# A two-layer encoder trunk on one core: projection weights in half loads, and the planner's tables dealt out anew

## The chip, the core and the metric

The kernel runs on one core of a Trainium2 chip. The metric is device time in microseconds for one launch. The core has five engines with instruction streams of their own: TensorE (PE, matmuls and, listed apart as PEld, weight loads), VectorE (DVE), ScalarE (ACT), GpSimd (POOL) and SyncE (SP). SP computes nothing here and issues DMAs, one after the other in the written order; POOL issues those DMAs that add into their target.

## The reference, cut to what matters

The input is 256 frames of 2048 features, all in float32. One layer of forgetting attention and one of chunked attention follow each other, each with an MLP.

```python
h = x
u = rms_norm(h, a_norm_g)                      # layer A
q, k, v, fz = split(u @ a_w_in)                # 16 heads of 128
q, k = rms_norm(q), rms_norm(k)                # per head
s = q k^T * 128**-0.5 + c_t - c_s              # c: running sum of log forget gates, causal
h = h + (softmax(s) @ v) @ a_w_out
h = h + relu(rms_norm(h) @ w1)**2 @ w2         # 2048 -> 8192 -> 2048
k, v = split(rms_norm(h, kv_norm_g) @ kv_w)    # shared keys and values, k normed per head
q = rms_norm(rms_norm(h, b_norm_g) @ b_w_q)    # layer B
h = h + (softmax(q k^T * 128**-0.5 + bias) @ v) @ b_w_out
h = h + relu(rms_norm(h) @ w1)**2 @ w2
```

## The kernel before, in words

**Units.** Every weight is read once, in pieces of 128 x 1024 called units; 972 of them in a fixed order make up the program. Each unit is split into a high part (`hi`, ACT, L287) and the rest (`lo`, DVE, L288), and PE multiplies hi and lo with the activations, which are split in the same way: three groups of four matmuls (L587, L589, L591). `fetch` (L341) keeps the splits AHEAD = 2 units before their matmuls.

**Loads.** `load` (L254) brings weights from DRAM into the pool `wraw` of three buffers of 1 MB, one DMA for a block of two units (L268). Only the first blocks of the program are cut smaller (`parts`, L274). `fetch` asks for blocks until EARLY = 2 blocks stand before their splits.

**Stages.** Layer A: for each of four groups of four heads a panel for Q, one for K and one for V (8 units each, 4 blocks); then the out-projection in four panels; then the MLP; then layer B's query projection; then K and V for layer B (two panels in each group), the second out-projection and the second MLP. MLP and query projection go in pairs of panels. A pair has seven forms f0 to f6 (sums of weight blocks times sums of activations, two steps of six matmuls each, half a unit) and plain units (a, b). The string in ORDER for each kind of pair says in which order forms and plain units come; `r` stands for a plain unit left over from the pair before. The sums of weights are made by adding DMAs on POOL (`add_on`, L317), by a bringing DMA on SP (`bring`, L306) and on DVE (`make`, L326), at places that BEHIND and OPENING set.

**Steps between the units.** All other work is hung behind units by a list, `fill`: after each unit `run_fill` runs the next entry, and `add_fill` and `deal` put work a number of units ahead. The tables are such numbers. HIDDEN places the hidden layer's four moves and six steps, LONG and SHORT the row statistics, the turning (L436), four moves (L451) and four steps of scaling, splitting and summing (L412 to L403) of a group of 512 features; LONG is for the end of layer A, SHORT for the out-projections. The engines DVE, ACT, PE and SP run in the written order (`keep_order`), so a place in the tables is a place in four queues.

**Attention.** `attend` (L782) puts the four heads of a group on steps `at`, and each head's values `far` steps later. Behind step `at` come the score matmuls (L744, L745), one step later bias and maximum on DVE, then the exponential on ACT, then norm and turning on DVE. Then SP writes the 128 x 384 probabilities to DRAM (`rows`, L462, turn<-pbuf) and four DMAs bring them back as columns (`columns`, L468, pbuf<-turn x4). The values (L776, L777) read them. In the table `at` is 9, 12, 15, 18 and `far` 9 for the first three groups, and 8, 10, 12, 13 and 8 for the last, whose values fall into the out-projection's first panel pair.

**Query steps.** `query` (L1020) sets the norms and scalings of layer B's queries by numbers in the code, and with them the flip of the row statistics and the second splitting of the activations for K and V.

Of the kernel before, what the change touches and what calls it, by code (L numbers as in the profile page):

```python
# [22 lines left out]
NG = H // GH  # L23
# [3 lines left out]
NEG = -1.0e30  # L27
UN = 1024
AHEAD = 2
EARLY = 2  # L30
HIDDEN = (
# [4 lines left out]
)  # L36
UA = UN // 512
LONG = (
# [4 lines left out]
)  # L43
SHORT = (
# [4 lines left out]
)  # L49
REL = 384  # L50
ORDER = {
# [9 lines left out]
}  # L61
BEHIND = {
    (0, 0): [(0, 1, "make", 0), (3, 1, "add", "T1", 0)],
    (0, 1): [(0, 1, "make", 1), (4, 1, "add", "T1", 1)],
    (1, 1): [(2, 0, "bring", "12", 0)],
    (3, 1): [(5, 0, "bring", "11", 0), (3, 0, "bring", "11", 1), (6, 0, "add", "T3", 1), (4, 0, "bring", "12", 1)],
    (2, 0): [(3, 0, "add", "T3", 0)],
}
SUBS = {"1": (2, 2), "2": (2, 2), "q": (2, 2)}
OPENING = (  # L70
    (23, "bring", "12", 0),
    (15, "bring", "12", 1),
    (5, "add", "T3", 0),
    (10, "add", "T3", 1),
    (6, "bring", "11", 0),
    (3, "bring", "11", 1),
)
BIG = 2 * UN
FORMS = ("11", "T3", "T2", "T1", "21", "T4", "22")
# [14 lines left out]
def trunk(ctx: ExitStack, tc: tile.TileContext, t):  # L94
# [53 lines left out]

    class Block:

        def __init__(self, src):
            self.src, self.raw = src, None

    def halves_of(src):
        return [(b, s) for b in map(Block, src) for s in range(2)]

    class Item:

# [76 lines left out]
            [(last - 2 + k, q) for k in range(2) for q in range(n)]  # L235

    def stage_units(src, tail):
        u = halves_of(src[i] for i in range(src.shape[0]))
# [8 lines left out]
    units.extend(halves_of(w_kv[i] for i in range(w_kv.shape[0])))  # L247
    tail_b = Tail(stage_units(w_ob, 4))
    plan_b = plan_mlp("b", None, tail_b)
    ready = deque()  # L250
# [3 lines left out]
    def load(parts=0):  # L254
        src, item = units.popleft(), None
        if isinstance(src, Item):
            item = src
            if item.u not in (4, 6):
                raws.append((item, None, (), 0))
                return  # L260
            block, s = item.pair.raw[item.u], item.s
        else:
            block, s = src
        new = block.raw is None
        if new:
            block.raw = wraw.tile([P, block.src.shape[1]], F32, name="raw", tag="raw")
            if not parts:
                SY.dma_start(block.raw, block.src)  # L268
        n = UN // (parts or 1)
        cuts = [slice(i * n, (i + 1) * n) for i in range(parts or 1)]  # L270
        raw = block.raw[:, half(s)]
        if parts:
            for c in cuts:
                SY.dma_start(raw[:, c], block.src[:, half(s)][:, c])  # L274
        raws.append((item, raw, cuts, new))

    def issue():
        if not raws:
            load()
        item, raw, cuts, _ = raws.popleft()  # L280
        if not cuts:
            assert (FORMS[item.u], item.s) in item.pair.done
            raw, cuts = item.pair.t[FORMS[item.u]][:, half(item.s)], [slice(0, UN)]
        hi = wsp.tile([P, UN], F32R, name="hi")
        lo = wsp.tile([P, UN], F32R, name="lo")
        for c in cuts:
            S.activation(hi[:, c], raw[:, c], AF.Copy)  # L287
            V.tensor_tensor(lo[:, c], raw[:, c], hi[:, c].bitcast(F32), op=ALU.subtract)  # L288
        ready.append((hi, lo))
        if item and item.u == 4:  # L290
            add_on(item.pair, "T4", item.s, raw)
        if item:
            item.pair.done.add((item.u, item.s))
            behind(item.pair, item.u, item.s)
        if later:
            for f in later.popleft():
                f()

    def half(s):
        return slice(s * UN, (s + 1) * UN)  # L300
# [5 lines left out]
            SY.dma_start(p.t[name][:, : p.subs * UN], p.big[name])  # L306
        p.done.add((name, s))

    def add_on(p, name, s, raw=None):
        to, block = {"T1": ("11", "12"), "T3": ("12", "22"), "T4": ("T2", "21")}[name]  # L310
        assert (to, s) in p.done
        assert {"T1": {(0, s), ("T2", s)}, "T3": set(), "T4": {(2, s)}}[name] <= p.done
        p.t[name] = p.t[to]
        p.done.add((name, s))
        d = p.t[name][:, half(s)]
        if raw is None:
            G.dma_start(d, p.big[block][:, half(s)], accum_op=ALU.add)  # L317
        else:
            V.tensor_tensor(d, d, raw, op=ALU.add)  # L319

    def make(p, s):
        assert (not p.prev or p.prev.did(5)) and {("T3", s), ("11", s)} <= p.done
# [459 lines left out]
    def attend(g, q, k, v, cq, o, make_bias):  # L782
        st = [{} for _ in range(GH)]
        box = {}
        k4 = k.rearrange("p (i a b c) -> p a b i c", i=4, a=GH, b=NB)
        at, far = ((8, 10, 12, 13), 8) if g == NG - 1 else ((9, 12, 15, 18), 9)
        items = [[] for _ in range(at[-1] + far + 1)]
        step = steps(lambda: make_bias(g, box))
        for i in (3, 6, 7):
# [230 lines left out]
    def query(g):  # L1020
        box = {}

        def f(b, ps):
            if b == 0:
                z, lq = turned(), landing(2 + g % 2)
                box["lq"], box["f"] = lq, head_norm(lambda: st2, z, lq, apart=(0, 2, None, None)[g])
            box["f"](b, ps)
            if b == NB - 1:
                add_fill([[]] * (7 + (2, 4, 0, 0)[g]) + [[lambda: qs.append(scale_q(box["lq"], 1, g))]])
                if g == 1:  # L1030
                    add_fill([[]] * 8 + [[st2.flip]])
                    slots = {0: 0, 1: 0, 2: 1, 3: 1, 4: 2, 5: 2, 6: 3, 7: 3}
                    add_fill([[again[slots[i]]] if i in slots else [] for i in range(8)])
        return f

    again = [steps(lambda n=n: kept[n](True, 2, xkv)) for n in range(NG)]
# [102 lines left out]
```

## Time and profile before

| | |
|---|---|
| runs, us | 2161.41, 2154.07, 2145.67 |
| median, us | 2154.07 |
| the profiled execution's own time, us | 2157.28 |
| its span, us | 2155.5 |
| mean granted clock of PE | 0.992 |
| bytes moved by DMA | 538.85 MB, mean 250 GB/s |

The span runs from the first to the last instruction, and 1.8 us lie around it. Times in timelines are microseconds from the start of the span. In a row of a timeline stand the start, the duration, the engine, the line, the operation, and in brackets the engine's idle time before it and what ended that; SPq is SP's queue of DMA issues, where a duration is time on SP and not the transfer. A row of the list of DMA issues ends with KB each and the median microseconds from issue to landing. Rows of the waits give a total in us, the number of times and the longest.

### The profile page before, as it was taken

The numbers are of one execution on the slowest core, as the hardware profiler recorded it, in microseconds if no ns is written. First come the engines' busy times: TensorE is split into PE (matmuls) and PEld (weight loads), VectorE is DVE, ScalarE is ACT, GpSimd is POOL, SyncE is SP. The second block draws the span as 40 slices with busy tenths as digits, with TensorE's granted clock in tenths as the row PEclk, the third lists the DMA queues.
The fourth block names the chain that finished last, engine by engine and source line by source line (L and its number), as shares of the span: only waits on it lengthen the run. The fifth ranks groups of instructions, "written<-read, shape, count | busy, mean of one in ns | idle before, by whom it ended". The sixth has DMA issues, their size and how long they took to land.

```text
span 2155.5 us, 26474 instructions
## 1 busy us (share of the span) xinstructions
PE 2093.5 (97%) x9114; PEld 1701.9 (79%) x9114; DVE 1735.8 (81%) x2003; ACT 1306.0 (61%) x1567; POOL 166.6 (8%) x184
## 2 busy tenths in 40 slices
PE   9999998999999999999989999989999999999999
PEld 7888886787887887887777888767878878878877
DVE  5767674899889889889898577648898898898896
ACT  6544543767567567557666445446675675675574
POOL 1101000001001000000002000000010010000000
PEclk9999999999999999999999999999999999999999
DMA  8776776888888888889786776758888888888884
GB/s 296 241 247 216 245 251 197 266 267 260 263 277 243 252 289 247 263 266 286 230 243 199 255 231 222 241 181 260 262 250 265 281 250 254 276 257 263 266 285 156
DMA packets 150678, 538.85 MB, mean 250 GB/s; under 512 B 41088, under 2 KB 78096, under 8 KB 101648
## 3 DMA queue, kind: packets, MB, share of 16 engines
q1 hardware_dynamic: 130960, 465.86, 60.5%
q0 software_dynamic: 19584, 71.31, 18.9%
q8 instruction: 71, 1.16, 0.2%
q14 instruction: 63, 0.52, 0.1%
HBM read 497.20 MB, written 15.75 MB: 238 GB/s over the span
## 4 chain that ended last, share of the span: by engine, by line
PE 81%; DVE 6%; DMA 5%; SPq 3%; ACT 3%; issue 2%; DVEq 0%; ACTq 0%; POOLq 0%
PE acc L587 17%; PE acc L589 17%; PE acc L591 17%; PE po L591 5%; PE po L587 5%; PE po L589 5%; PE s L589 4%; PE s L591 4%; PE s L587 4%; DVE lo L288 3%; SPq L451 3%; ACT hi L287 1%; DMA q<-z 1%; DMA pbuf<-turn 1%; DMA turn<-pbuf 1%
## 5 line engine op out<-in xcount | busy, mean ns | idle before, releaser
L288 DVE TENSOR_TENSOR lo<-raw,hi 128x1024 fp32r<-128x1024 f32 (+1 forms) x634 | 759.3, 1214 | 206.0 <-ACT hi L287 202.7
L287 ACT ACTIVATE hi<-raw 128x1024 fp32r<-128x1024 f32 (+1 forms) x634 | 658.5, 1053 | 365.7 <-PE acc L589 199.0
L587 PE MATMUL acc<-hi,act 128*128 128x512 f32 x1644 | 468.3, 401 | 18.9 <-ACT hi L287 9.8
L589 PE MATMUL acc<-hi,act 128*128 128x512 f32 x1644 | 452.9, 392 | 0.0
L591 PE MATMUL acc<-lo,act 128*128 128x512 f32 x1644 | 451.4, 391 | 0.9 <-DVE lo L288 0.9
L587 PEld LDWEIGHTS acc<-hi,act 128*128 128x128 f32 x1644 | 308.4, 190 | 89.7 <-ACT hi L287 13.5
L589 PEld LDWEIGHTS acc<-hi,act 128*128 128x128 f32 x1644 | 311.3, 189 | 67.3 <-DVE act L382 1.1
L591 PEld LDWEIGHTS acc<-lo,act 128*128 128x128 f32 x1644 | 309.3, 189 | 68.6 <-DVE lo L288 3.7
L287 ACT ACTIVATE hi<-w 128x1024 fp32r<-128x1024 f32 x204 | 214.6, 1056 | 104.4 <-PE po L589 52.0
L288 DVE TENSOR_TENSOR lo<-w,hi 128x1024 fp32r<-128x1024 f32 x204 | 245.5, 1221 | 34.5 <-ACT hi L287 32.7
L287 ACT ACTIVATE hi<-wT 128x1024 fp32r<-128x1024 f32 x136 | 142.3, 1057 | 65.0 <-PE po L589 24.9
L288 DVE TENSOR_TENSOR lo<-wT,hi 128x1024 fp32r<-128x1024 f32 x136 | 162.7, 1221 | 20.9 <-ACT hi L287 20.3
L587 PE MATMUL s<-hi,act 128*128 128x512 f32 x476 | 136.4, 391 | 6.5 <-ACT hi L287 4.1
L591 PE MATMUL s<-lo,act 128*128 128x512 f32 x476 | 139.0, 397 | 2.6 <-DVE lo L288 2.6
L589 PE MATMUL s<-hi,act 128*128 128x512 f32 x476 | 136.7, 392 | 1.1 <-DVE act L416 1.1
L587 PEld LDWEIGHTS s<-hi,act 128*128 128x128 f32 x476 | 89.2, 188 | 27.2 <-ACT hi L287 5.3
L591 PEld LDWEIGHTS s<-lo,act 128*128 128x128 f32 x476 | 88.3, 189 | 28.2 <-DVE lo L288 10.8
L589 PEld LDWEIGHTS s<-hi,act 128*128 128x128 f32 x476 | 89.4, 188 | 21.1 <-DVE act L416 2.4
L319 DVE TENSOR_TENSOR wT<-wT,raw 128x1024 f32<-128x1024 f32 x68 | 82.9, 1219 | 0.0
L326 DVE TENSOR_TENSOR wT<-w,w 128x1024 f32<-128x1024 f32 x68 | 82.9, 1219 | 0.0
L779 ACT ACTIVATE act<-po 128x256 fp32r<-128x256 f32 x32 | 12.3, 385 | 102.1 <-PE po L777 102.1
L587 PE MATMUL po<-hi,act 128*128 128x512 f32 x272 | 73.1, 391 | 0.0
(181 smaller groups left out, 2221.6 us busy)
## 6 DMA issues: line engine op xcount, KB each, us to landing
raw<-in_w_in SPq DMA_DIRECT2D x46, 1024.0 KB, 6.2
raw<-in_s1a SPq DMA_DIRECT2D x32, 1024.0 KB, 6.1
raw<-in_s2a SPq DMA_DIRECT2D x32, 1024.0 KB, 7.0
raw<-in_w_kv SPq DMA_DIRECT2D x32, 1024.0 KB, 5.8
raw<-in_s1b SPq DMA_DIRECT2D x32, 1024.0 KB, 5.8
raw<-in_s2b SPq DMA_DIRECT2D x32, 1024.0 KB, 6.2
q<-z SPq DMA_DIRECT2D x672, 32.0 KB, 4.1
raw<-in_w_oa SPq DMA_DIRECT2D x16, 1024.0 KB, 7.1
```

What stands on the lines that cost most here:

```text
L287: S.activation(hi[:, c], raw[:, c], AF.Copy)
L288: V.tensor_tensor(lo[:, c], raw[:, c], hi[:, c].bitcast(F32), op=ALU.subtract)
L319: V.tensor_tensor(d, d, raw, op=ALU.add)
L326: V.tensor_tensor(p.t["T2"][:, half(s)], p.t["T3"][:, half(s)], p.t["11"][:, half(s)], op=ALU.add)
L451: SY.dma_start(d[32 * j : 32 * j + 32, i], z[32 * i : 32 * i + 32, j * n : (j + 1) * n])
L587: TE.matmul(ps, xh, cut(hi, j), start=first, stop=False, **kw)
L589: TE.matmul(ps, xl, cut(hi, j), start=False, stop=False, **kw)
L591: TE.matmul(ps, xh, cut(lo, j), start=False, stop=last, **kw)
L779: S.activation(o[i][:, 0], po[:, :T], AF.Copy)
```

## The change

Weights of the QKV, KV and both output projections are loaded in halves of a block, one DMA of 512 KB for each unit, into the same three buffers of 1 MB; the MLP's and the query's blocks stay whole. EARLY is 4 and counts a half as 1 and a whole block as 2; the first panel's own look-ahead (1) now is a half. The steps of attention and of the query projection become tables (ATT, BIAS, QUERY, AGAIN); BIAS keeps its numbers. T4's sum now is made where BEHIND says, and no more with its block's split. All other tables have new numbers, of which a few stand here:

```diff
-EARLY = 2
+EARLY = 4
 LONG = (
-    (3, 0, 0, 1, 1, 1, 6, 7, 7, 7),
+    (1, 0, 0, 0, 0, 1, 6, 6, 6, 9),
...
 SHORT = (
...
-    (7, 0, 0, 1, 2, 5, 9, 10, 13, 13),
+    (8, 0, 0, 1, 2, 5, 6, 10, 14, 14),
...
+QUERY = (0, 1, 13, 12, 6, 17, 6)
+AGAIN = (0, 1, 2, 3, 5, 5, 7, 7)
+ATT = ((8, 14, 18, 18, 10), (8, 9, 12, 12, 9))
+BIAS = (3, 6, 7)
 ORDER = {
...
-    "q0": "r f0 f1 f2 f3 f4 r a a f5 b f6 b",
-    "q1": "f0 f1 f2 f4 r r a f5 r r a f3 b b f6",
+    "q0": "f0 r f1 r r f2 f3 f4 a a f5 f6 b b",
+    "q1": "f0 f1 r f2 r f4 a f5 r r a r f3 b b f6",
...
-        def __init__(self, src):
-            self.src, self.raw = src, None
+        def __init__(self, src, whole=True):
+            self.src, self.raw, self.whole = src, None, whole
...
-    units.extend(halves_of(w_in[i] for i in range(w_in.shape[0])))
+    units.extend(halves_of((w_in[i] for i in range(w_in.shape[0])), False))
...
-        if parts:
+        if not block.whole:
             for c in cuts:
                 SY.dma_start(raw[:, c], block.src[:, half(s)][:, c])
-        raws.append((item, raw, cuts, new))
+        elif new:
+            SY.dma_start(block.raw, block.src)
+        raws.append((item, raw, cuts, 2 * new if block.whole else 1))
...
-            add_on(item.pair, "T4", item.s, raw)
+            item.pair.t["21", item.s] = raw
...
-        at, far = ((8, 10, 12, 13), 8) if g == NG - 1 else ((9, 12, 15, 18), 9)
+        *at, far = ATT[g == NG - 1]
...
-                add_fill([[]] * (7 + (2, 4, 0, 0)[g]) + [[lambda: qs.append(scale_q(box["lq"], 1, g))]])
+                add_fill([[]] * QUERY[2 + g] + [[lambda: qs.append(scale_q(box["lq"], 1, g))]])
                 if g == 1:
-                    add_fill([[]] * 8 + [[st2.flip]])
+                    add_fill([[]] * QUERY[6] + [[st2.flip]])
+                    deal(AGAIN, [again[i // 2] for i in range(8)])
```

Lines of the kernel after stand 7 lower for most (L268 and L274 become L279, L462 becomes L469, L468 becomes L475). Three places show the order on the engines.

SP at the end of the first attention, where the last group's four heads go out (turn<-pbuf) and come back (pbuf<-turn), between loads for the out-projection (raw). Before:

```order
98 L462 DMA turn<-pbuf 128x384
99 L306 DMA w_2685<-in_f1a 128x2048
100 L468 DMA pbuf<-turn 32x4x96 x4
101 L268 DMA raw<-in_w_oa 128x2048
102 L462 DMA turn<-pbuf 128x384
103 L468 DMA pbuf<-turn 32x4x96 x4
104 L268 DMA raw<-in_w_oa 128x2048
105 L462 DMA turn<-pbuf 128x384
106 L468 DMA pbuf<-turn 32x4x96 x4
107 L462 DMA turn<-pbuf 128x384
108 L268 DMA raw<-in_w_oa 128x2048
109 L468 DMA pbuf<-turn 32x4x96 x4
```

And after:

```order
99 L469 DMA turn<-pbuf 128x384
100 L313 DMA w_2743<-in_f1a 128x2048
101 L279 DMA raw<-in_w_oa 128x1024
102 L475 DMA pbuf<-turn 32x4x96 x4
103 L469 DMA turn<-pbuf 128x384
104 L279 DMA raw<-in_w_oa 128x1024
105 L475 DMA pbuf<-turn 32x4x96 x4
106 L279 DMA raw<-in_w_oa 128x1024 x2
107 L469 DMA turn<-pbuf 128x384 x2
108 L279 DMA raw<-in_w_oa 128x1024
109 L475 DMA pbuf<-turn 32x4x96 x8
```

The last two heads go out one behind the other and come back in one run of eight, and each load between is half as large.

PE in the first query pair, at its forms f0 (s<-hi,act) and f1 (po<-hi,S). Before:

```order
1518 L587 MATMUL s<-hi,act 128x512 x2
1519 L589 MATMUL s<-hi,act 128x512 x2
1520 L591 MATMUL s<-lo,act 128x512 x2
1521 L587 MATMUL po<-hi,S 128x512 x2
1522 L589 MATMUL po<-hi,S 128x512 x2
1523 L591 MATMUL po<-lo,S 128x512 x2
```

And after:

```order
1515 L594 MATMUL s<-hi,act 128x512 x2
1516 L596 MATMUL s<-hi,act 128x512 x2
1517 L598 MATMUL s<-lo,act 128x512 x2
1518 L594 MATMUL acc<-hi,act 128x512 x4
1519 L596 MATMUL acc<-hi,act 128x512 x4
1520 L598 MATMUL acc<-lo,act 128x512 x4
1521 L594 MATMUL po<-hi,S 128x512 x2
```

A plain unit of the last w2 pair (acc) has moved between the two forms; before, it stood ahead of both.

DVE shortly before, in the last w2 pair, where the first group's activations for the query pairs are split (act) and summed (sum, S). Before:

```order
763 L634 TENSOR_TENSOR acc<-acc,p_8437 128x512
764 L288 TENSOR_TENSOR lo<-raw,hi 128x1024 x2
765 L416 TENSOR_TENSOR act<-y,act 128x1024
766 L394 TENSOR_TENSOR sum<-y 128x256
767 L395 TENSOR_TENSOR sum<-y,sum 128x256
768 L396 TENSOR_TENSOR sum<-y 128x256
769 L397 TENSOR_TENSOR sum<-y,sum 128x256
770 L403 TENSOR_TENSOR S<-sum,S 128x512 x2
771 L288 TENSOR_TENSOR lo<-raw,hi 128x1024 x4
```

And after:

```order
758 L641 TENSOR_TENSOR acc<-acc,p_8480 128x512
759 L295 TENSOR_TENSOR lo<-raw,hi 128x1024
760 L423 TENSOR_TENSOR act<-y,act 128x1024
761 L401 TENSOR_TENSOR sum<-y 128x256
762 L402 TENSOR_TENSOR sum<-y,sum 128x256
763 L403 TENSOR_TENSOR sum<-y 128x256
764 L404 TENSOR_TENSOR sum<-y,sum 128x256
765 L295 TENSOR_TENSOR lo<-raw,hi 128x1024 x4
766 L410 TENSOR_TENSOR S<-sum,S 128x512 x2
```

The group's split and sums stand one weight split earlier, and the split of the sums (S) four weight splits later.

More of the change, by code (lines that the diff above doesn't have):

```diff
@@ L71 @@
     (23, "bring", "12", 0),
-    (15, "bring", "12", 1),
-    (5, "add", "T3", 0),
-    (10, "add", "T3", 1),
+    (17, "bring", "12", 1),
+    (4, "add", "T3", 0),
+    (9, "add", "T3", 1),
     (6, "bring", "11", 0),
-    (3, "bring", "11", 1),
+    (1, "bring", "11", 1),
 )
@@ L149, in trunk, with halves_of @@
     class Block:
-        def __init__(self, src):
-            self.src, self.raw = src, None
-    def halves_of(src):
-        return [(b, s) for b in map(Block, src) for s in range(2)]
+        def __init__(self, src, whole=True):
+            self.src, self.raw, self.whole = src, None, whole
+    def halves_of(src, whole=True):
+        return [(b, s) for b in (Block(i, whole) for i in src) for s in range(2)]
     class Item:
@@ L237, in stage_units @@
     def stage_units(src, tail):
-        u = halves_of(src[i] for i in range(src.shape[0]))
+        u = halves_of((src[i] for i in range(src.shape[0])), False)
         u[:16] = [u[8 * q + i] for i, q in steps_of(2)]
@@ L243, in trunk @@
     n_out = 4 * KT // UA - 4
-    units.extend(halves_of(w_in[i] for i in range(w_in.shape[0])))
+    units.extend(halves_of((w_in[i] for i in range(w_in.shape[0])), False))
     tail_a = Tail(stage_units(w_oa, 4))
     plan_a = plan_mlp("a", "qb", tail_a)
-    units.extend(halves_of(w_kv[i] for i in range(w_kv.shape[0])))
+    units.extend(halves_of((w_kv[i] for i in range(w_kv.shape[0])), False))
     tail_b = Tail(stage_units(w_ob, 4))
@@ L307, in bring, with add_on @@
         p.done.add((name, s))
-    def add_on(p, name, s, raw=None):
+    def add_on(p, name, s):
         to, block = {"T1": ("11", "12"), "T3": ("12", "22"), "T4": ("T2", "21")}[name]
         assert (to, s) in p.done
-        assert {"T1": {(0, s), ("T2", s)}, "T3": set(), "T4": {(2, s)}}[name] <= p.done
+        assert {"T1": {(0, s), ("T2", s)}, "T3": set(), "T4": {(2, s), (4, s)}}[name] <= p.done
         p.t[name] = p.t[to]
@@ L315, in add_on @@
         d = p.t[name][:, half(s)]
-        if raw is None:
+        if name == "T4":
+            V.tensor_tensor(d, d, p.t["21", s], op=ALU.add)
+        else:
             G.dma_start(d, p.big[block][:, half(s)], accum_op=ALU.add)
-        else:
-            V.tensor_tensor(d, d, raw, op=ALU.add)
     def make(p, s):
```

23 lines of the change are left out of this document (11 added, 12 removed), and 34 rows, old and new, of tables (HIDDEN, LONG, ORDER, SHORT).

## Prediction, made before the changed kernel ran

> **What bounds the kernel now.** I read the busy times first, then who TensorE (PE) waits for, then a table of stretches, and only then the timelines of the places that these named. The page and its list of DMA issues:
>
> ```profile
> PE 2093.5 (97%) x9114; PEld 1701.9 (79%) x9114; DVE 1735.8 (81%) x2003; ACT 1306.0 (61%) x1567; POOL 166.6 (8%) x184
> ...
> L288 DVE TENSOR_TENSOR lo<-raw,hi 128x1024 fp32r<-128x1024 f32 (+1 forms) x634 | 759.3, 1214 | 206.0 <-ACT hi L287 202.7
> ...
> raw<-in_w_in SPq DMA_DIRECT2D x46, 1024.0 KB, 6.2
> ```
>
> ```profile
> w<-in_f1a POOLq DMA_DIRECT2D x32, 512.0 KB, 6.0
> ```
>
> PE is busy for 97% of the span of 2155.5 us, so all its idle time is 62 us. No matmul is removed or added. What the change can give is therefore part of these 62 us, and of the time in which PE is busy at a lowered clock. It has no more than that to give, but it can add new waits. PE's waits, largest first (total us, times, longest):
>
> ```profile
> PE po L776 <- DMA pbuf<-turn: 12.3, 5, 3.3
> PE po L587 <- DVE s L632: 11.3, 9, 2.5
> PE acc L587 <- ACT hi L287: 9.8, 6, 2.8
> PE acc L587 <- DVE acc L632: 4.4, 8, 0.6
> ```
>
> The largest is the attention's values waiting for their turned probabilities. No row of PE's waits names a weight load, so the weight loads by themselves are hidden. Three stretches of 25 us (PE busy, PEld, DVE, ACT, POOL, clock, DMA share, GB/s):
>
> ```profile
> 325.00:350.00 25.00, 19.79 (x76) 15.43 (x75) 8.95 (x11) 6.72 (x9) 0.00 (x0) 0.86 0.67 222
> 1075.00:1100.00 25.00, 20.11 (x87) 15.71 (x86) 23.84 (x24) 16.49 (x22) 3.47 (x4) 1.00 0.81 212
> 1400.00:1425.00 25.00, 20.00 (x76) 15.23 (x75) 8.72 (x11) 6.37 (x9) 0.00 (x0) 0.86 0.62 208
> ```
>
> The first and the last are the ends of the two attentions: DVE and ACT are two thirds idle, PE waits, and the clock falls to 0.86. The middle one is the first query pair: DVE is busy 23.84 of 25 us, so there DVE is the bound. These are two different illnesses, and the change touches both.
>
> **Attention tables (ATT) and halves, first attention.** PE at its end (start, duration, and in brackets the idle time):
>
> ```profile
> 318.67 1.07 PE L591 MATMUL acc<-lo,act 128*128 128x512 f32 x4
> ...
> 321.15 1.08 PE L589 MATMUL acc<-hi,act 128*128 128x512 f32 x4
> ...
> 324.79 1.07 PE L591 MATMUL acc<-lo,act 128*128 128x512 f32 x4
> 329.05 1.19 PE L776 MATMUL po<-pbuf,kv 128*128 128x256 f32 x2 [3.19 <-DMA pbuf<-turn]
> ...
> 332.08 1.07 PE L589 MATMUL acc<-hi,act 128*128 128x512 f32 x4
> ...
> 339.11 1.07 PE L591 MATMUL acc<-lo,act 128*128 128x512 f32 x4
> 342.15 1.14 PE L776 MATMUL po<-pbuf,kv 128*128 128x256 f32 x2 [1.98 <-DMA pbuf<-turn]
> ...
> 345.63 1.09 PE L589 MATMUL acc<-hi,act 128*128 128x512 f32 x4
> ```
>
> Without a wait, the way from one L591 over a head's values to the next L589 takes 321.15 - 318.67 = 2.48 us. With the two waits it takes 7.29 and 6.52 us, so they cost 4.81 + 4.04 = 8.85 us, though the idle time is only 3.19 + 1.98 = 5.17: the rest, a factor of 1.71, is the lowered clock behind each wait. The Trainium skill ("TensorE: Matmul & The Clock Gate", Part 1) has the clock go down only after an idle window of some 3.4 us, which none of these waits reaches; by that the two would cost their 5.17 us and no more, and the forecast would lie some 7 us higher. The rows differ, and I go by the rows.
>
> The waits come from SP, which issues in order (start, time in SP):
>
> ```profile
> 306.29 0.33 SPq L462 DMA_DIRECT2D turn<-pbuf  x1
> ...
> 313.77 1.75 SPq L468 DMA_DIRECT2D pbuf<-turn  x4
> ...
> 316.09 0.38 SPq L462 DMA_DIRECT2D turn<-pbuf  x1
> 322.30 2.08 SPq L468 DMA_DIRECT2D pbuf<-turn  x4
> 324.49 0.45 SPq L268 DMA_DIRECT2D raw<-in_w_oa  x1
> 325.03 0.38 SPq L462 DMA_DIRECT2D turn<-pbuf  x1
> 331.56 1.74 SPq L468 DMA_DIRECT2D pbuf<-turn  x4
> 333.40 0.38 SPq L462 DMA_DIRECT2D turn<-pbuf  x1
> ...
> 335.39 1.75 SPq L468 DMA_DIRECT2D pbuf<-turn  x4
> ```
>
> Each head goes out to DRAM (L462) and comes back in columns (L468), and the second row can't be issued before the first has landed. Everything behind it on SP waits too, the next head's way out above all. So four journeys stand in a row: 7.48, 6.21, 6.53 and 1.99 us. The 1.99 is the one with no weight load of 1 MB right ahead of it.
>
> After the change heads 2 and 3 go out in two rows back to back and come back together: three waits in a row, not four. Worked out for head 1 with nothing faster: way out at 313.77 + 1.75 = 315.5, back from 321.7 to 323.8, and landed as long after that as now (329.05 - 324.38 = 4.67) at 328.5. PE wants it at 329.05 - 3.19 = 325.9, since its place (step 18) is kept, so 2.6 us of wait would stay. With each journey behind half a load taking about 4 us (between 1.99 and 6.53) it lands near 323 and nothing waits. Heads 2 and 3 then leave at about 321, land at 325 to 327.5, have eight rows to issue (2 x 1.75), and are there at 332 to 336; PE wants them at 342.15 - 1.98 - 4.81 = 335.4. I take 0.9 us of wait as what stays, times 1.71 is 1.5: **gain 7.3 us**, between 4.4 (2.6 x 1.71 stays) and 8.85.
>
> **The same at the second attention.** Its three waits, and the worst journey there:
>
> ```profile
> 1369.01 0.67 PE L776 MATMUL po<-pbuf,kv 128*128 128x256 f32 x2 [2.24 <-DMA pbuf<-turn]
> ...
> 1404.39 0.67 PE L776 MATMUL po<-pbuf,kv 128*128 128x256 f32 x2 [1.62 <-DMA pbuf<-turn]
> ...
> 1417.74 1.19 PE L776 MATMUL po<-pbuf,kv 128*128 128x256 f32 x2 [3.31 <-DMA pbuf<-turn]
> ```
>
> ```profile
> 1398.69 0.38 SPq L462 DMA_DIRECT2D turn<-pbuf  x1
> 1407.15 1.74 SPq L468 DMA_DIRECT2D pbuf<-turn  x4
> ```
>
> Together 7.17 us, by the factor of 1.71 some 12.3 us. The first is the third group's second head; its values move from step 21 to 24 while its score moves from 12 to 14, one unit more room (2.73 us: four groups of matmuls from 321.15 to 324.79 are 0.91 us each, a unit is three), so it goes. The others are the fourth group as above; the third journey of 8.46 us falls away with the pairing, but if the pair's own journey took as long, about 3.5 us of wait would stay, 6.0 with the factor. I take 1.6 as what stays: **gain 10.7 us**, between 6.3 and 12.3.
>
> **Query pairs (ORDER, QUERY, AGAIN, LONG).** PE in the first query pair, and behind the second one's forms:
>
> ```profile
> 1080.71 0.73 PE L591 MATMUL po<-lo,S 128*128 128x512 f32 x2 [1.81 <-DVE lo L288]
> ...
> 1088.07 0.70 PE L587 MATMUL po<-hi,S 128*128 128x512 f32 x2 [2.55 <-DVE s L632]
> ```
>
> ```profile
> 1124.48 1.20 PE L587 MATMUL s<-hi,act 128*128 128x512 f32 x4 [0.32 <-ACT hi L287]
> ...
> 1126.30 1.19 PE L589 MATMUL s<-hi,act 128*128 128x512 f32 x4 [0.62 <-DVE act L416]
> ```
>
> A form step feeds PE for half a unit (1.36 us) and takes 1.21 us of DVE for its split, so five forms in a row leave DVE no room for anything else. In the first query pair plain units now stand between f0, f1 and f2, which relieves DVE by half a unit each; but LONG puts a whole group's scaling, sums and splits on one step, and the last group's residual and its turning come later, into the forms. The work is the same, the place is full. It could take away both waits (-4.4 us) or add as much again (+4.4). I take **+1.5 us**, near the middle because DVE's total doesn't change, above it because work moves into the forms. In the second query pair the two waits above go, since a plain unit now stands behind f1 and f2: 0.94 us of wait and half as much in slowed matmuls, **gain 1.4 us** (0 to 2).
>
> **What costs nothing, and its cover.** Halves: about 110 blocks (QKV, KV, both out-projections) issue one DMA more each, at 0.45 us of SP (row 324.49); SP mostly waits for a buffer there, and that is the cover. Look-ahead counts halves, 4 for 2, so each half is asked for four units before its split as the first half is now. The raw buffers are freed by the block as before. The steady MLP pairs keep the order on DVE and ACT around their waits (the rows of 11.3 and 4.4 us), so these stay, plus or minus 2 us in all. BEHIND and OPENING shift loads and adding loads on SP and POOL; POOL is 8% busy, and each of them waits for its data and not for its turn. The scaling of the queries and the flip (QUERY, AGAIN) come a few units earlier or later than now, long before the panel that reads them, which covers them; without that cover a scaling costs ACT about one split. SHORT takes the scaling in the second panel of the out-projections three units earlier, right behind four moves on SP; if ACT waits for them, 2 us in each layer, and if not, nothing: I take **+1.0 us** for both.
>
> **Sum.** -7.3 - 10.7 + 1.5 - 1.4 + 1.0 = -16.9 us on the profiled execution's 2157.28 gives 2140.4. That execution lies 3.2 us above the median of the runs shown (2154.07), so the forecast is 2137 us. All terms at their good ends give 2124, all at their bad ends 2154, which are the first two rivals; half of the way to each, 2130 to 2146, is the forecast's own range.
>
> **Rivals.**
> *The halves help further.* Small transfers all queue behind less, all waits at the attentions go (21.2 us), both waits of the first query pair go and their clock with them (4.4 x 1.6 = 7), and 2 at the second: 2157.3 - 30 is 2127, less 3.2 is 2124. For it: the 1.99 us journey. Against it: DVE's 23.84 of 25.
> *Given back.* Halves land no sooner: POOL's loads of 512 KB take 6.0 us to land, SP's of 1 MB take 6.2. Then the attentions give only 4.4 + 6.3 = 10.7, the first query pair costs 4.4 more, and the out-projections 4: -2.3, or 2152. The change would then not do what its first part says.
> *Slower: loads become the bound.* A block's two halves feed PE for 2 x 2.73 = 5.46 us, while a whole load takes 6.2 us to land and PE still never waits for one: loads overlap. If halves overlap less well, each of the 80 blocks of the QKV and KV panels is late by some time x. From x = 0.2 us the gain of 16.9 is eaten; at 0.5 us it is +40 - 17, or 2177. Against it: the DMA share of 0.62 to 0.67 in the table, with room left.
> The Trainium skill ("DMA: Bandwidth & Descriptors", Rules for kernel authors) wants 1 MiB or more in each DMA, and its fit (Anatomy of one DMA), 2.0 us and then 436 KB per us, gives by estimate 3.2 us a half and 6.4 a block, nearly 1 us over the 5.46 if loads went one after the other, some 75 us in all. Against that rule stands the same row: 6.2 us for a whole load is over 5.46 already, and nothing waits.
>
> **Chances.** The forecast 0.45, further gain 0.24, given back 0.23, slower 0.08. About 1% is what a measurement of this kernel can tell from no change: under 2132.5 is faster, over 2175.6 slower. The further gain is faster in nearly all cases, and so is a fifth of the forecast's own range: faster 0.32. Slower is the last rival: 0.08. The same: 0.60. The range goes from 2120, most of the further gain, to 2158, most of what is given back.
>
> **What would show it.** Right: the wait of L776's successor on pbuf falls from 12.3 us under 3, the clock in the two attention stretches is 1.00, two rows of the way out stand back to back, PE doesn't wait for a raw load, and the waits in the second query pair go. Wrong: journeys of 6 us and more behind half loads; a split's wait for raw in the QKV panels; a longer row of waits for DVE in the first query pair.

## The result, and the profile after

The changed kernel takes 2155.20 us (median of 20 runs, 2150.54 to 2160.72), the kernel before in 20 runs 2154.12 us (2145.67 to 2161.41). The ratio is 1.0009, with a 95% interval of 0.9997 to 1.0021: no change that can be told from none. The forecast was 2137.

The profiled execution of the changed kernel took 2150.54 us, which is 4.7 us below its kernel's median; that of before, 2157.28, was 3.2 us above its own. So the two traces differ by 6.7 us in a direction that the medians don't confirm. That turns out to be half of the story.

The busy times of the changed kernel, a row of its list of DMA issues, and PE's waits (total us, times, longest):

```profile
PE 2086.3 (97%) x9114; PEld 1697.6 (79%) x9114; DVE 1738.3 (81%) x2003; ACT 1305.8 (61%) x1567; POOL 168.5 (8%) x184
```

```profile
raw<-in_w_in SPq DMA_DIRECT2D x94, 512.0 KB, 5.9
```

```profile
PE acc L594 <- ACT hi L294: 16.2, 8, 4.2
PE s L594 <- ACT hi L294: 11.2, 5, 4.7
PE po L594 <- DVE s L639: 10.5, 9, 1.7
PE acc L594 <- DVE acc L639: 4.4, 8, 0.6
```

In the kernel before the second of these rows was

```profile
PE s L587 <- ACT hi L287: 4.1, 3, 2.2
```

The attention's row, 12.3 us before, has gone altogether. The two rows for ACT's hi, which before were 9.8 and 4.1 us, are 16.2 and 11.2 now. What was won at one place has turned up at another. In front of ACT, its scaling steps' waits for the moves have doubled; here is that row of the changed kernel, and then that of the kernel before:

```profile
ACT y L419 <- DMA q<-z: 32.6, 6, 7.2
```

```profile
ACT y L412 <- DMA q<-z: 16.4, 4, 7.0
```

Stretches of 25 us of the changed kernel (PE, PEld, DVE, ACT, POOL, clock, DMA share, GB/s):

```profile
315.00:340.00 25.00, 24.85 (x114) 20.51 (x113) 14.54 (x20) 9.76 (x13) 0.00 (x0) 1.00 0.90 265
365.00:390.00 25.00, 20.76 (x85) 16.75 (x84) 17.09 (x19) 14.71 (x24) 1.72 (x2) 0.93 0.79 232
415.00:440.00 25.00, 21.13 (x88) 17.09 (x87) 16.64 (x16) 13.44 (x16) 1.72 (x2) 0.93 0.84 289
1068.00:1093.00 25.00, 21.32 (x89) 16.00 (x88) 24.55 (x29) 18.51 (x29) 3.48 (x4) 1.00 0.76 209
1385.00:1410.00 25.00, 24.85 (x114) 20.52 (x113) 14.92 (x23) 9.69 (x12) 0.00 (x0) 1.00 0.89 263
1435.00:1460.00 25.00, 21.38 (x87) 17.19 (x87) 16.83 (x17) 14.70 (x23) 1.70 (x2) 0.93 0.81 236
1490.00:1515.00 25.00, 20.32 (x84) 16.47 (x83) 16.59 (x15) 14.58 (x17) 1.71 (x2) 0.93 0.83 264
```

The first and the fifth are the two attention ends, now at full clock and with PE busy throughout; before they read 19.79 and 20.00 at a clock of 0.86. The other rows but the fourth are four stretches in the out-projections and the first w1 pairs, with PE idle part of the time behind an ACT and a DVE that are themselves busy for only 54 to 68% of it: they are stopped, not full. The fourth is the first query pair, as DVE-bound as before.

From the starts of the units' first matmuls in the two traces one can add up where the time is (units are numbered from 0 to 971; 96 is the first out-projection's first, 588 belongs to the second's; the last pairs are counted up to the start of unit 971):

| units | before, us | after, us | difference |
|---|---|---|---|
| 104-111, 588-603: the attention ends | 96.70 | 76.37 | -20.3 |
| 112-145, 604-639: out-projections' second halves, first w1 pairs | 172.40 | 186.34 | +13.9 |
| 460-523: last w2 pair of layer A, query pairs | 138.05 | 136.59 | -1.5 |
| 146-459, 640-971: the other MLP pairs | 1233.28 | 1238.15 | +4.9 |
| all others | | | -3.8 |

**Where the time came from.** SP at the end of the first attention (start, time in SP):

```profile
303.24 0.33 SPq L469 DMA_DIRECT2D turn<-pbuf  x1
...
306.63 2.22 SPq L475 DMA_DIRECT2D pbuf<-turn  x4
308.96 0.40 SPq L469 DMA_DIRECT2D turn<-pbuf  x1
309.69 0.35 SPq L279 DMA_DIRECT2D raw<-in_w_oa  x1
314.10 1.98 SPq L475 DMA_DIRECT2D pbuf<-turn  x4
...
317.49 1.08 SPq L469 DMA_DIRECT2D turn<-pbuf  x2
...
325.61 3.64 SPq L475 DMA_DIRECT2D pbuf<-turn  x8
```

Three journeys of 3.39, 5.14 and 8.12 us stand where four of 7.48, 6.21, 6.53 and 1.99 were. The pair's journey is long, and PE has no wait for it in this trace.

**Where it went.** SP, ACT and PE behind the second panel of the first out-projection:

```profile
360.35 1.54 SPq L279 DMA_DIRECT2D raw<-in_w_oa  x3
361.93 2.47 SPq L458 DMA_DIRECT2D q<-z  x4
```

```profile
369.99 0.91 ACT L419 ACTIVATE y<-q,gsb 128x256 f32<-128x256 f32 x2 [7.18 <-DMA q<-z]
370.80 1.99 ACT L294 ACTIVATE hi<-raw 128x1024 fp32r<-128x1024 f32 x2
```

```profile
371.89 2.07 PE L594 MATMUL acc<-hi,act 128*128 128x512 f32 x4 [4.24 <-ACT hi L294]
373.77 1.65 PE L596 MATMUL acc<-hi,act 128*128 128x512 f32 x4
```

The four moves leave SP at 364.40 and land 5.6 us later. The scaling step (L419), which SHORT has put three units earlier, stands at the head of ACT's queue all that time, 7.18 us. Two splits that have nothing to do with it stand behind, and PE runs out of split weights: 4.24 us idle, and then four matmuls in 2.07 us, not 1.07. The same happens behind the first w1 pair, where the moves of the last groups now start in one run of twelve:

```profile
405.10 7.49 SPq L458 DMA_DIRECT2D q<-z  x12
...
413.27 2.41 SPq L458 DMA_DIRECT2D q<-z  x4
```

```profile
419.42 1.70 ACT L419 ACTIVATE y<-q,gsb 128x256 f32<-128x256 f32 x4 [3.50 <-DMA q<-z]
```

```profile
423.20 2.08 PE L594 MATMUL s<-hi,act 128*128 128x512 f32 x4 [3.87 <-ACT hi L294]
```

### The profile page after: what moved, and what is told of

It is laid out like the page before. It is cut to its first block, busy times and chain, and to the rows that moved or that the text cites. A ratio compares the mean times of both kernels' runs of the same rounds, so it can differ in the third digit from the quotient of the medians.

```text
span 2148.8 us, 26598 instructions
## 1 busy us (share of the span) xinstructions
PE 2086.3 (97%) x9114; PEld 1697.6 (79%) x9114; DVE 1738.3 (81%) x2003; ACT 1305.8 (61%) x1567; POOL 168.5 (8%) x184
## 4 chain that ended last, share of the span: by engine, by line
PE 79%; DVE 8%; DMA 5%; issue 3%; SPq 3%; ACT 2%; ACTq 0%; DVEq 0%
PE acc L596 17%; PE acc L594 17%; PE acc L598 16%; PE po L598 5%; PE po L594 5%; PE po L596 5%; PE s L598 4%; PE s L594 4%; PE s L596 4%; DVE lo L295 4%; SPq L458 2%; ACT hi L294 2%; DMA q<-z 2%; DMA raw<-in_s2a 1%; DVE wT L324 1%
## 5 line engine op out<-in xcount | busy, mean ns | idle before, releaser
L294 ACT ACTIVATE hi<-wT 128x1024 fp32r<-128x1024 f32 x136 | 142.3, 1057 | 59.8 <-PE acc L596 20.3
L594 PE MATMUL s<-hi,act 128*128 128x512 f32 x476 | 138.5, 396 | 11.4 <-ACT hi L294 11.2
L594 PE MATMUL po<-hi,act 128*128 128x512 f32 x272 | 72.8, 389 | 0.0
L596 PE MATMUL po<-hi,act 128*128 128x512 f32 x272 | 72.7, 389 | 0.0
```

Of the source, the lines that this page charges most:

```text
L594: TE.matmul(ps, xh, cut(hi, j), start=first, stop=False, **kw)
L596: TE.matmul(ps, xl, cut(hi, j), start=False, stop=False, **kw)
```

## The experiments

They ran on three chips on which the kernel before takes 2145 to 2151 us, against 2154 us in the result. So each is given as its ratio to runs of before on the same chip, with the 95% interval. The changed kernel itself was run only for the result; its variant with whole loads was run beside the others. The theory: the attention tables win what the profile shows, and SHORT gives it back. The rivals: the half loads crowd the moves; the MLP's tables cost; the attention's waits in the first profile were not typical.

| run | ratio to before | interval |
|---|---|---|
| the changed kernel (result) | 1.0009 | 0.9997-1.0021 |
| changed, SHORT undone | 0.9962 | 0.9949-0.9976 |
| before, attention tables alone | 0.9977 | 0.9965-0.9988 |
| the same again | 0.9972 | 0.9959-0.9986 |
| before, half loads alone | 0.9979 | 0.9961-0.9996 |
| before, attention tables and half loads | 0.9966 | 0.9953-0.9978 |
| before, SHORT alone | 1.0038 | 1.0023-1.0054 |
| changed, whole loads | 1.0005 | 0.9994-1.0015 |
| changed, SHORT's second group undone | 0.9981 | 0.9963-0.9999 |
| changed, SHORT's last two groups undone | 1.0016 | 1.0001-1.0032 |
| changed, SHORT and MLP tables undone | 0.9953 | 0.9936-0.9970 |
| the same, first group's scaling later | 0.9961 | 0.9942-0.9979 |
| the same, and the last group's too | 1.0047 | 1.0024-1.0070 |

Each of these runs also left a trace, and so did three more of the kernel before (below). The stretches of the result's table can be measured in all of them. The attention ends take 79.95 to 96.70 us in the six traces with the old attention tables, and 76.37 to 78.09 in the eleven with the new ones. The second row (units 112-145 and 604-639) takes 171.05 to 173.84 us in the ten traces with SHORT as before, and 181.62, 181.89 and 186.34 in the three with all its new rows. So the gain and the loss sit where the two profiles have them, in every trace. The query stretch is 140.4 us on average in nine traces with the old query tables and 138.7 in eight with the new. The other MLP pairs differ by 0.8 us on average between the old MLP tables (eleven traces, without the last version of all) and the new (five), in favour of the old, which is far within the spread of single traces.

### SHORT undone, SHORT alone

```diff
 SHORT = (
-    (3, 0, 0, 0, 0, 0, 3, 3, 5, 5),
-    (8, 0, 0, 1, 2, 5, 6, 10, 14, 14),
-    (1, 0, 2, 2, 2, 3, 8, 10),
-    (0, 0, 1, 1, 1, 3, 5, 5),
+    (5, 0, 0, 0, 0, 0, 3, 3, 5, 7),
+    (7, 0, 0, 1, 2, 5, 9, 10, 13, 13),
+    (1, 0, 0, 2, 3, 4, 9, 10),
+    (0, 0, 0, 1, 2, 3, 5, 5),
```

> The changed kernel with the table SHORT of the kernel before, all else as changed. Theory (the attention gain of about 21 us is real and SHORT gives most of it back, because ACT's second scaling step of the second group waits for the last of its four moves): faster than before by 12 to 18 us, about 2140, and the two waits of PE of 4.2 and 3.6 us behind ACT's hi in the out-projections gone. Rival (the moves land late because half loads crowd the queues, whatever SHORT says): no better than 2150. Rival (the MLP's tables are what costs): 2150 too.

Measured: 2136.25 us beside 2145.43, ratio 0.9962. The direction is the theory's, and the waits of 4.2 and 3.6 us are gone; but against before it is 8 us, not 12 to 18.

The opposite, the rows of the changed kernel put into the kernel before:

> The kernel before with the table SHORT of the changed one alone. Theory: 9 to 15 us slower than before (2163 to 2169), with the wait of ACT for the moves in the second panel. Rival (SHORT costs only in the company of half loads): within 3 us of before.

Measured: 2153.91 us beside 2145.43, ratio 1.0038, 8.5 us slower. That is just under the forecast's 9 us, and the rival, within 3 us, is out. SHORT costs 8 us alone and about 10 in the changed kernel (1.0009 against 0.9962): within the intervals, its cost is the same in whole and in half loads.

### The attention tables alone, twice

```diff
-        at, far = ((8, 10, 12, 13), 8) if g == NG - 1 else ((9, 12, 15, 18), 9)
+        at, far = ((8, 9, 12, 12), 9) if g == NG - 1 else ((8, 14, 18, 18), 10)
```

> The kernel before with the two attention tables of the changed one alone, whole loads. Theory: the pairing of heads and one unit more of room take most of the waits of L776 away, 12 to 18 us faster (2136 to 2142). Rival (it needs the halves, since each way out stands behind a load of 1 MB): half of that or less, 2146 or more.

Measured: 2140.92 us beside 2145.43, ratio 0.9977: 5 us. In the trace no wait of L776 is left. So the tables do what they were forecast to do, without the halves, and it is worth a quarter of what the two profiles show. The mechanism is the theory's; the size, less than half of 12 to 18 us, is the rival's.

> The kernel before with the attention tables alone, a second time, to tell how much they give. Theory (the waits of L776 cost 8 to 10 us in an ordinary execution and the tables take them all): ratio 0.9955 to 0.9965. Rival (part of it is given back elsewhere, as the first run of this kernel had it): ratio 0.9975 to 0.998.

Measured: 0.9972, 6 us. In this trace one wait of L776 is left:

```profile
PE po L776 <- DMA pbuf<-turn: 1.5, 1, 1.5
```

The ratio lies between the two forecasts. The two runs of this kernel agree with each other, so the gain is 5 to 6 us.

### The kernel before, three more profiles

> The kernel before itself once more, for its profile. Theory (the waits of L776 for the turned probabilities vary from execution to execution, and the first profile had an unlucky one): the waits come to 2 to 8 us in place of 12.3, and the two attention ends are shorter than in the first profile by as much as the pairing gave there. Rival (they are a fixed cost of that kernel): 11 to 13 us again.

> The kernel before, a third profile. Theory (the waits for the turned probabilities vary between executions): 2 to 8 us of waits of L776, and the execution's time goes up and down with them. Rival (the first profile's 12.3 us are typical): 11 us or more.

> The kernel before, a fourth profile, as the third: 2 to 8 us of waits of L776 by the theory, 11 us or more by the rival.

The row of L776 in these three executions, which took 2151.42, 2146.06 and 2157.82 us, and in the execution of SHORT alone, whose attention code is that of before:

```profile
PE po L776 <- DMA pbuf<-turn: 7.3, 4, 2.4
```

```profile
PE po L776 <- DMA pbuf<-turn: 7.0, 4, 2.7
```

```profile
PE po L776 <- DMA pbuf<-turn: 6.1, 6, 2.9
```

```profile
PE po L776 <- DMA pbuf<-turn: 3.9, 4, 1.8
```

The first profile had 12.3. From the units' starts the attention ends are 10.4, 9.0, 7.9 and 4.4 us longer in these four than in the changed kernel, against 20.3 in the first. So the theory holds for the size of the waits: one and the same kernel pays anything from 8 to 20 us there, and with the new rows of SHORT beside the same attention code 4 us. The chip is not held apart in this: the record names none for the session of the result, from which the first profile comes, and the three others come from two chips. What doesn't hold is that the whole execution follows these waits: the one of 6.1 us is the slowest of the three. It spends 8.75 us more than the first profile in the second layer's MLP pairs. The largest piece of that is an idle time of PE of 4.30 us at unit 756. ACT waited there for 5.06 us, at a step of the hidden layer, for the last of a run of twelve moves, which took SP 10.93 us (9.00 in the first profile) and landed 4.4 us later (2.3). The executions of a kernel differ at several places at once.

### Half loads

Changed, with whole loads (only the first two blocks in halves, as before):

```diff
-    units.extend(halves_of((w_in[i] for i in range(w_in.shape[0])), False))
+    units.extend(halves_of((w_in[i] for i in range(2)), False) + halves_of(w_in[i] for i in range(2, w_in.shape[0])))
...
-        u = halves_of((src[i] for i in range(src.shape[0])), False)
+        u = halves_of(src[i] for i in range(src.shape[0]))
...
-    units.extend(halves_of((w_kv[i] for i in range(w_kv.shape[0])), False))
+    units.extend(halves_of(w_kv[i] for i in range(w_kv.shape[0])))
```

> The changed kernel with all blocks loaded whole but the first two, as before. Theory (halves matter little, tables do): within 4 us of the changed kernel, 2151 to 2159. Rival (halves crowd the moves and lose time): 2145 or less. Rival (halves carry the attention gain): 2163 or more, with waits of L783 back.

Measured: ratio 1.0005, the same as with halves (1.0009). In the changed kernel the halves neither cost nor bring anything that these runs can tell, about 2 us either way.

Before, with halves alone (the loading code of the changed kernel, every table as before, so that PE, DVE and ACT keep their order):

> The kernel before with half loads alone, the orders of PE, DVE and ACT as before. Theory (each journey stands behind half as much): the waits of L776 fall below the 6 to 12 us of the four profiles of before, 1 to 4 us faster. Rival (a load of 512 KB lands as late as one of 1 MB beside the rest of the traffic): within 1 us of before. Rival (the transfers become the bound): slower by 10 us and more, with PE waiting behind loads.

Measured: ratio 0.9979, 4.5 us faster by the ratio, with an interval that nearly reaches 1. Which wait they shorten isn't shown. The attention's, in this trace, reads

```profile
PE po L782 <- DMA pbuf<-turn: 3.4, 3, 1.8
```

That is less than in the four profiles of before (6.1 to 12.3), but with whole loads and the new SHORT it was 3.9.

Halves and the attention tables together:

> The kernel before with the attention tables and the half loads of the changed one, every other table as before. Theory (the halves shorten the journeys and with the pairing take all waits of L776): ratio 0.995 to 0.9965, better than the attention tables alone (0.9977). Rival (halves do nothing here; the query tables are what adds to the attention tables): ratio 0.9975 to 0.9985.

Measured: ratio 0.9966, 7 us, and 0.3 us of the wait is left in the trace. The single ratios would add up to 10 us or so, which the interval just allows (0.9953). That both take away the same wait would explain the 7, but the runs don't show it.

### Which rows of SHORT

The second group's row of before in the changed kernel:

```diff
-    (8, 0, 0, 1, 2, 5, 6, 10, 14, 14),
+    (7, 0, 0, 1, 2, 5, 9, 10, 13, 13),
```

> The changed kernel with one row of SHORT as before, that of the second group (its second scaling step nine units behind its panel again, not six). Theory (this one step is most of what SHORT costs: ACT waits there for the last move, and PE behind it 4.2 and 3.6 us, slowed clock on top): 6 to 10 us faster than the changed kernel, ratio to before 0.996 to 0.998. Rival (the rows of the last two groups cost as much, since their moves stand in one run of twelve): half of that, ratio 0.9985 to 1.

Measured: ratio 0.9981, 6 us better than the changed kernel: just outside the theory's 0.996 to 0.998, and the interval reaches over most of the rival's 0.9985 to 1 as well. ACT's step now has its data when it comes up, with no wait in front:

```profile
369.86 0.90 ACT L419 ACTIVATE y<-q,gsb 128x256 f32<-128x256 f32 x2
```

PE's waits behind the first w1 pairs stay: 4.41 and 4.49 us in this trace.

The rows of the third and the fourth group of before in the changed kernel:

```diff
-    (1, 0, 2, 2, 2, 3, 8, 10),
-    (0, 0, 1, 1, 1, 3, 5, 5),
+    (1, 0, 0, 2, 3, 4, 9, 10),
+    (0, 0, 0, 1, 2, 3, 5, 5),
```

> The changed kernel with the rows of SHORT of the third and fourth group as before. Theory: PE's waits behind the first w1 pair (3.9 and 4.7 us) fall to 1.6 and 2.2 as before, 3 to 5 us faster than the changed kernel, ratio to before 0.9985 to 0.9995; the waits of the second group stay. Rival (the second group's step is all of it): the ratio stays at 1.0009.

Measured: ratio 1.0016, no gain; a miss. PE's wait of 3.87 us fell to 1.71, but a new one of 3.05 us stands a few units ahead of it. SP and ACT there (L281 is the load of a whole block in the changed kernel):

```profile
406.38 0.54 SPq L281 DMA_DIRECT2D raw<-in_f1a  x1
406.96 3.74 SPq L458 DMA_DIRECT2D q<-z  x4
```

```profile
414.45 2.00 ACT L294 ACTIVATE hi<-raw 128x1024 fp32r<-128x1024 f32 x2 [7.18 <-DMA raw<-in_f1a]
```

This weight load left SP only at 406.38, behind four moves (at 394.65 in the changed kernel, ahead of all of them), and the split waited for it for 7.18 us. In these two arrangements the late moves hurt either way: in front of ACT's scaling, or in front of a weight load. The rival's ratio came, but not its reason, since the second group's row alone gave 6 of the 10 us. How the rest splits, with the first group's row in it, no run shows.

### Versions that might beat both

SHORT and the MLP's tables (HIDDEN, BEHIND, OPENING and the orders of the w1 and w2 pairs) as before, the rest as changed:

> The changed kernel with SHORT, HIDDEN, BEHIND, OPENING and the orders of the MLP's pairs as before: attention tables, halves, LONG and the query tables stay. Theory (the MLP's new tables cost some 3 us in the steady pairs, as the two profiles have it): 2 to 4 us faster than the changed kernel with SHORT alone undone, ratio 0.9945 to 0.995. Rival (that difference is noise between executions): ratio 0.996 as there. Rival (the MLP's tables carry a gain): 0.9975 or more.

Measured: 2136.07 us beside 2145.98, ratio 0.9953. It has the lowest ratio of all runs, 10 us below the kernel before and, by its own ratio of 1.0009, some 12 below the changed one. It isn't told apart from SHORT undone alone (0.9962); the MLP tables cost at most a few us.

From this kernel, the first group's scaling two units later:

```diff
-    (5, 0, 0, 0, 0, 0, 3, 3, 5, 7),
+    (5, 0, 0, 0, 0, 0, 5, 5, 7, 8),
```

> The kernel with the attention tables, halves and query tables of the change and SHORT and the MLP's tables of before (0.9953 of before), and in SHORT the first group's four steps at 5, 5, 7, 8 in place of 3, 3, 5, 7. Theory (what the out-projection loses is ACT standing at a scaling step whose moves have not landed): PE's waits of 2.2 and 2.9 us behind ACT's hi in the first panel go, 4 to 8 us faster than that kernel, ratio 0.9915 to 0.9935. Rival (the wait moves to the next place that needs the same data): ratio 0.995.

Measured: ratio 0.9961, no gain; the rival was right. ACT and SP of this kernel at this place (its lines stand one lower than the changed kernel's):

```profile
355.17 1.06 ACT L293 ACTIVATE hi<-raw 128x1024 fp32r<-128x1024 f32 x1 [6.61 <-DMA raw<-in_w_oa]
```

```profile
340.74 10.10 SPq L457 DMA_DIRECT2D q<-z  x16
350.94 0.53 SPq L278 DMA_DIRECT2D raw<-in_w_oa  x1
```

With the scaling out of the way, ACT stands just as long at the next split (6.42 us at the scaling in the kernel that it comes from), since SP needs 10 us to issue sixteen moves and the next weight load can't leave before. The queue that binds here is SP's, and ACT's row named only the first of two things that were late because of it.

Then the last group's scaling two units later too, with units of b ahead of those of a that read it:

```diff
-    "first": "f0 r r r f1 r f2 a f3 a f4 f5 f6 a a b b",
+    "first": "f0 r r r f1 r f2 a f3 a f4 f5 f6 b b a a",
...
-    (0, 0, 0, 1, 2, 3, 5, 5),
+    (0, 0, 0, 1, 2, 3, 7, 7),
```

> The same as the run with later scaling, and in the first w1 pair the units of b ahead of the last two of a, with the last group's scaling two units later (7, 7 for 5, 5). Theory: the waits of 2.1 and 2.8 us at that pair go too, another 4 to 7 us, ratio 0.9885 to 0.9915. Rival (the hidden layer's steps, which start two units later, wait in their turn): no better than the run with later scaling alone.

Measured: ratio 1.0047, slower; a miss. PE waits 4.00 us at unit 146 for the last group's activations, whose scaling was moved back, and ACT now waits for weight loads in and behind this pair:

```profile
420.93 1.06 ACT L293 ACTIVATE hi<-raw 128x1024 fp32r<-128x1024 f32 x1 [6.22 <-DMA raw<-in_s1a]
...
459.87 1.06 ACT L293 ACTIVATE hi<-raw 128x1024 fp32r<-128x1024 f32 x1 [6.40 <-DMA raw<-in_s1a]
```

The second of these loads left SP at 454.38, behind another run of sixteen moves, which took 14.57 us.

## Why the prediction was wrong

**The attention tables, forecast -7.3 and -10.7 us.** The mechanism was right: three journeys in a row in place of four, one unit more of room, and no wait of L776 left. The size was wrong by a factor of three: 5 and 6 us in two runs, 7 with the halves. The failed step is to take the five waits of one execution, 12.3 us, for the kernel's, and to multiply them by 1.71. Three other executions of this kernel show 6.1 to 7.3, and one with the new SHORT 3.9. The sum did see that this execution lay 3.2 us above the median and took that off at its end; taken off this term instead, it would have given 2140, which is still far off. The spread of the three times shown, 2145.67 to 2161.41, was nearly as large as the whole gain.

**The factor of 1.71 for the lowered clock.** There is no such factor. Between the start and the end of the span, the granted clock in all seventeen traces is either 1.00 or 0.50, and it is 0.50 for spells of 3.41 us, or of two times that. The first profile behind its two waits in the first attention:

```profile
328.55:331.96 3.41, 2.91 (x8) 2.47 (x9) 0.42 (x1) 1.23 (x2) 0.00 (x0) 0.50 0.62 250
342.20:345.61 3.41, 3.36 (x8) 2.42 (x9) 0.91 (x2) 1.33 (x2) 0.00 (x0) 0.50 0.66 274
```

A spell costs about half its length, 1.7 us, whatever the wait was. The first profile has 17.06 us of spells in its attention ends: 12.3 and half of 17.06 are 20.8 us, where 20.3 was measured. The three other profiles of this kernel have 6.83, 3.41 and 3.41 us of them, which gives 10.7, 8.7 and 7.8 us for the measured 10.4, 9.0 and 7.9; the execution of SHORT alone has none, 3.9 for 4.4. Whether a wait brings a spell is partly chance. The same wait of 2.17 us in the first out-projection, in the first profile and in the fourth:

```profile
366.14 2.08 PE L587 MATMUL acc<-hi,act 128*128 128x512 f32 x4 [2.17 <-ACT hi L287]
```

```profile
358.09 1.21 PE L587 MATMUL acc<-hi,act 128*128 128x512 f32 x4 [2.17 <-ACT hi L287]
```

Over all seventeen traces, idle times of PE from 0.4 to 1.6 us had a spell begin in them or just behind them once in 461 cases, those of 1.6 to 3.2 us in 61 of 135, and the 20 longer ones always. By the Trainium skill ("TensorE: Matmul & The Clock Gate", Part 1) waits of 2 to 3 us would have no such tail; the first profile's have one.

**SHORT, forecast +1.0 us with 2 us in each layer as its end.** This is the other term that failed: 8.5 us alone, 10 in the changed kernel. With the attention's shortfall of 11 us it makes up the 18 us between forecast and result. The step named the right place, the right engine and the right cause, and set the price without a row. What it left out is what stands behind the step: ACT's queue stops until the last of four moves has landed, and behind a stopped ACT stand the splits, of which PE has two in store. In the changed kernel's trace 7.18 us on ACT became 4.24 us on PE, so the store covered 2.9, and behind that comes the slowed clock.

**The halves, forecast as no cost and as shorter journeys.** Half right. They cost nothing that runs can tell, and the rival of loads as the bound didn't come. That no row of PE's waits names a load says little, in the prediction too: a split always stands between, so the load shows in ACT's waits. There the splits of the four matrices in question wait 27.6 us for their loads in the profile before and 7.2 in the one after, and none of that reached the time (1.0005 with whole loads). In the kernel before the halves bring some 4.5 us (0.9979). Why nothing of it is left beside the new tables is not shown; that the tables had already taken the same waits is the likeliest reading. One sign against them came and did no harm: the pair's journey behind half loads took 8.12 us.

**The query pairs, forecast +1.5 and -1.4 us.** The stretch of units 460 to 523 is 1.5 us shorter in the changed profile, and 1.8 us shorter on average over all traces, where the sum of the two terms was near nothing. The waits in the second query pair are gone as forecast. By the runs' ratios this can't be told from nothing.

**The rest.** The rival called "given back" has the time right, 2152, and its cause wrong: it had the halves land no sooner and the attention's gain small for that. But the gain was small since the loss was small, and what was given back was given back by SHORT. In ratios: -7 us for attention tables and halves, +8 for SHORT alone, and about -1 for the other tables (SHORT undone against attention tables and halves) leave nothing; the result is +1 to +2, within the intervals. That the rival's time fits is luck.

**The signs.** All five signs that the prediction named for being right are there in the profile: no wait for the probabilities, full clock at both attention ends, the two ways out back to back, no PE row that waits for a load, and no waits in the second query pair. The time did not move all the same. None of the signs looked at the scaling steps of the out-projections, where SHORT puts its cost.

What stays open: why the waits of L776 differ so much between executions of one kernel (the chip, as said, is not held apart), why the same run of moves is slower in one execution than in another, and which row of SHORT but the second costs the rest.

## What to carry to other kernels

A wait that hangs on how long a small DMA stands in a queue varies from execution to execution: take its size from several profiles. Price the lowered clock behind waits by its spells in the trace, not by a factor on the waits. A step on an in-order engine that is moved ahead of its data costs everything queued behind it; price it as the issue time of the last transfer, plus its landing, less the work that the next engine has in store, and name a sign that would show it. Where moving such a step only brings up another wait, look for the queue that makes both late, here SP with sixteen moves in 10 us.

## What the runs showed that was not expected

Halving a load saved little of its time to landing: 6.2 us became 5.9 for the QKV weights and 5.8 became 5.7 for KV. In the two out-projections 7.1 became 5.7 and 7.2 became 6.0; but in the four profiles of the kernel before the first takes 6.4 to 7.1 and the second 5.9 to 7.2, so only a part of that can be put down to the halves. The Trainium skill ("DMA: Bandwidth & Descriptors", Anatomy of one DMA) gives by estimate 3.2 against 4.4 us for one load at a time, from a fit to DMAs that GpSimd issues, while these come from SP; beside other traffic its figures do not show here, and the extra DMAs cost nothing that runs can tell. The small moves (32 KB) are dear at the other end: 0.63 us of SP each (10.10 us for sixteen), against 0.35 us for a load of 512 KB (the row at 309.69; 0.53 us right behind a run of moves).
